# Chunk products of a state-space mixer placed in column groups of the array

## The chip, the cores and the metric

The kernel runs on one core of a Trainium2 chip. Its engines are TensorE (PE, with the weight loads shown apart as PEld), VectorE (DVE), ScalarE (ACT), GpSimd (POOL) and SyncE (SP, which issues most transfers). They run their own instruction streams in order and wait for each other by semaphores. The metric is the device time of one execution in microseconds; three timed runs of the kernel before gave 1025.63, 1027.56 and 1028.41 us, median 1027.56 us.

## The reference

One layer of a decoder for 512 tokens and 1024 features: a half-step SwiGLU, a mixer in which eight attention heads with forget gates and a diagonal state-space model (SSM) work side by side, a second half-step SwiGLU, a gated embedding and a final norm. The change is in the SSM alone: 32 groups of 16 channels, each with 64 complex states.

```python
abar_r = decay * jnp.cos(dt * ai)
abar_i = decay * jnp.sin(dt * ai)
...
bu_r = jnp.einsum('blgh,gph->blgp', u, bbar_r)
bu_i = jnp.einsum('blgh,gph->blgp', u, bbar_i)
...
_, _, xr, xi = lax.associative_scan(_ssm_combine, (a_r_full, a_i_full, bu_r, bu_i), axis=1)
y = (jnp.einsum('blgp,ghp->blgh', xr, c_re.astype(f32))
     - jnp.einsum('blgp,ghp->blgh', xi, c_im.astype(f32))
     + d_skip.astype(f32) * u)
y = jax.nn.gelu(y.reshape(B, L, SSM_WIDTH)).astype(s.dtype)
return y * jax.nn.sigmoid(y @ w_glu + b_glu)
```

## The kernel before

Most of the program is dense work: some 3800 matrix products of a 128x128 weight block with 512 columns (lines 236 to 238: each product of float32 numbers is three products of high and low parts), and some hundreds with 256 columns. `run` goes through a list of units. A unit has two steps, here called slots; in a slot ACT rounds the weights that are used two slots later to their high part `whi` (line 160), evictions and other chains issue their work, DVE makes the low part `wlo` (line 75), and PE does some twelve products. A unit's results are evicted in the next slot. Chains are generators. They are advanced twice in a slot, once ahead of the slot's products (their work for ACT and DVE) and once behind them (their work for PE), so that the code fixes each engine's order.

The SSM is computed in 64 chunks of 8 tokens. `ssm_prep` builds its matrices from the parameters during the first SwiGLU: `m1` (chunk inputs to states), `m2` (states to chunk outputs) and `m3` (chunk inputs to outputs of the same chunk). For `m3` it makes four batches of eight groups. In a batch, eight products (line 668) of a 16-column stationary block with 128 moving columns fill partitions 0 to 15 of two PSUM banks, two ACT copies (line 672) bring them to `kt`, and transfers spread `kt` to `m3`.

`ssm_chain` runs beside the products of the token units and the first query and key units. It turns the inputs into chunk form (line 720), multiplies to states (line 745: the two groups of a pair go to partitions 0 to 63 and 64 to 127 of the result), rotates and scans them on DVE (`rotate`, in two halves of 16 groups, whose last step is the four ACT copies `st` of line 788), and then treats four feature tiles of eight groups. `tile_chain` does this for a tile: `outputs` (16 products with 64 stationary columns and 128 moving ones, lines 797 and 798, in partitions 0 to 63 of two banks), `collect` (one bank copied by ACT, line 808, the other by DVE, line 810, to `yt`), `features` (eight transposes of 64 partitions, line 816), and the GELU in three parts (`gelu_a` begins with a copy on ACT, line 825). `TILES` lists the steps at which the four tiles begin: 4, 5, 7 and 8.

At these steps ACT and DVE have other work queued as well: the forget gate (`fz`, `fn`, `fc`, with a change of the activation table before and behind it), the values `v` of the attention (line 81 on ACT, line 78 on DVE), from whose PSUM banks the next unit takes its own, and then the queries, keys and softmax (`attention`).

Of the kernel before, what the change touches and what calls it, by code (L numbers as in the profile page):

```python
# [29 lines left out]
TILES = [4, 5, 7, 8]  # L30
# [12 lines left out]
def hybrid_trunk_kernel(ctx: ExitStack, tc: tile.TileContext, xT, pT, w13a, w2a, w13b, w2b, wqk, wv, ws, wf,  # L43
                        wglu, wout, wgate, wproj, cols, bf, ssm_s, ssm_bc, dskip, outT, dbg=None):
    nc = tc.nc
    V, S, G, T = nc.vector, nc.scalar, nc.gpsimd, nc.tensor
# [43 lines left out]
    # ---- constants  # L90
# [14 lines left out]
    # the activation table and the tensor engine's clock come up while x arrives  # L105
# [4 lines left out]
    # 0 | 1e30 above the diagonal  # L110
# [5 lines left out]
    # operands of the scores by head of the pair: (hi of q | selector of the head) and  # L116
    # (hi of k | cumulative gates of all heads), the head's own half of the partitions first
# [4 lines left out]
    # ---- dense work: a list of units; each has up to two weight halves of [128, 512], the matrix products that  # L122
    # use them in two steps, and what follows on the other engines
    class Unit:
        def __init__(self, srcs, steps, posts=(), need=None, alloc=None, ahead=True):
            # posts: (step it follows, slots to wait, function); need: what they wait for besides
# [47 lines left out]
    def run_posts(posts):  # L174
        # what waited for the first norm comes a few at a time
# [12 lines left out]
    def convert(u, nxt, h):  # L188
        # the next unit's half h of the weights, and what else is to be taken ahead
# [50 lines left out]
    def gemm_steps(box, key, rhs, n, half=None):  # L240
        # sum over n blocks of stationary weights against rhs(k) -> (hi, lo), in two steps; half: where both steps
        # find their weights, each in its own unit
# [11 lines left out]
    # ---- x*g -> hi, lo; squares summed; 1/rms by token  # L254
    class Norm:
# [36 lines left out]
        def scaled(self, src, scol, slots=2):  # L292
            # x*g/rms -> hi, lo, once the chain has run
# [41 lines left out]
    # ---- macaron half step  # L335
    PARTS = [range(0, 7), range(7, 14), range(14, 22)]

    def ffn_units(nrm, w13, w2, final, skip_first=False):
        units = []
        ready = lambda: nrm.r is not None  # L340
        for pi, part in enumerate(PARTS):
            hid = {}
            for f in part:
# [30 lines left out]
                if f == 0:  # L374
                    # side by side: the last blocks of the input come late
# [18 lines left out]
            # the first two go on side by side: the hidden parts that they need last come late  # L394
# [19 lines left out]
    # ---- SSM matrices from the parameters  # L414
    # "pair" layout: (group in pair, state) on partitions, 16 pairs on the free dim
    # "stack" layout: (real | imaginary, state) on partitions, 32 groups on the free dim
    def ssm_prep(M):
# [50 lines left out]
        # rotation tables e^{i phi c}, phi = 8 dt Im(a), c = 0..63  # L468
# [72 lines left out]
        # powers of abar, j = 0..8  # L541
# [7 lines left out]
        n = 1  # L549
# [17 lines left out]
        # zero-order-hold input matrix  # L567
# [46 lines left out]

        yield
        yield
        # chunk input matrices: [(s', h), (re | im, state)]
        m1 = []
        ps = None

# [940 lines left out]
```

## Time and profile before

| what | value |
|---|---|
| timed runs | 1025.63, 1027.56, 1028.41 us |
| profiled execution | span of 1025.1 us from the first to the last instruction; no other time of it is listed |
| PE, DVE, ACT busy | 99 %, 65 %, 41 % of the span |
| mean granted TensorE clock | 0.996 of full speed |

A busy share is an average over the whole span. The profile's row of the span in 40 slices shows where it differs: DVE is at nine tenths or more from about 460 to 540 us, and at five or six tenths in the long dense stretches. "PE busy" counts the time in which at least one product is under way; products overlap, so the time from the start of one to the start of the next is what counts. The chain of waits gives just that: in it each product has the time by which it delayed the end. A product of float32 operands with 128 or 64 columns shows as two records, called passes here, because the array goes over it twice; a transpose shows as one.

### The profile page before, as it was taken

The page shows a single profiled execution, that of the slowest core. Times are in us where ns is not written, and L with a number is a line of the kernel's source. Part 1 is how long each engine was busy: PE and PEld are TensorE (multiplying, and loading weights), DVE is VectorE, ACT ScalarE, POOL GpSimd, SP SyncE. Part 2 cuts the span into 40 slices and gives each one's busy share as a digit, 9 for nine tenths or more (in the row PEclk, how much of TensorE's full clock was granted, in tenths as well). Part 3 has the DMA queues.
Part 4 walks back from the last instruction along what each step waited for, and adds up shares of the span by engine and source line. Part 5 has one row for each costly group of instructions (what it writes and reads, how often), then busy time and mean ns, then how long its engine had stood idle before and what let it go on. Part 6 is the DMA issues. An engine that isn't in the chain of part 4 may idle for free.

```text
span 1025.1 us, 13779 instructions
## 1 busy us (share of the span) xinstructions
PE 1013.1 (99%) x5004; PEld 852.0 (83%) x5004; DVE 663.3 (65%) x1319; ACT 421.5 (41%) x793; POOL 45.6 (4%) x52
## 2 busy tenths in 40 slices
PE   9999999999999999999999999999999999999996
PEld 7888888888878889888888888888888888888896
DVE  6678687767645561879998975553455446655465
ACT  6333233322333352468897443332333224434332
POOL 0430000001000001001000000000000000000000
PEclk9999999999999999999999999999999999999998
DMA  6423332233244331212212232333333334533102
GB/s 207 151 88 96 108 96 93 77 99 103 83 105 117 103 92 52 63 53 83 73 52 75 88 96 86 100 88 100 100 103 88 98 103 150 168 93 104 32 1 82
DMA packets 58244, 96.06 MB, mean 94 GB/s; under 512 B 10224, under 2 KB 17008, under 8 KB 58176
## 3 DMA queue, kind: packets, MB, share of 16 engines
q1 hardware_dynamic: 57920, 94.63, 30.5%
q8 instruction: 39, 0.64, 0.3%
q0 software_dynamic: 256, 0.56, 0.2%
q14 instruction: 29, 0.24, 0.1%
HBM read 91.89 MB, written 2.10 MB: 92 GB/s over the span
## 4 chain that ended last, share of the span: by engine, by line
PE 96%; ACT 2%; DVE 1%; DMA 0%; SPq 0%; issue 0%; POOL 0%; DVEq 0%; ACTq 0%
PE ps L236 30%; PE ps L237 29%; PE ps L238 29%; PE ps L1439 1%; PE ps L797 1%; PE ps L668 1%; PE ps L798 1%; PE ps L1075 1%; PE ps L327 1%; PE ps L316 0%; ACT lg L81 0%; DMA x<-xT 0%; PE ps L1038 0%; PE ps L1039 0%; PE ps L745 0%; PE ps L1121 0%
## 5 line engine op out<-in xcount | busy, mean ns | idle before, releaser
L236 PE MATMUL ps<-xhl,whi 128*128 128x512 f32 x816 | 320.5, 393 | 0.0
L238 PE MATMUL ps<-xhl,whi 128*128 128x512 f32 x816 | 317.8, 389 | 0.0
L237 PE MATMUL ps<-xhl,wlo 128*128 128x512 f32 x816 | 317.8, 389 | 0.0
L160 ACT CAST whi<-wraw 128x512 fp32r<-128x512 f32 x324 | 196.1, 607 | 240.1 <-PE ps L238 177.8
L75 DVE TENSOR_TENSOR wlo<-wraw,whi 128x512 fp32r<-128x512 f32 x324 | 216.2, 673 | 11.0 <-ACT whi L160 10.7
L236 PEld LDWEIGHTS ps<-xhl,whi 128*128 128x128 f32 x816 | 153.2, 188 | 32.4 <-ACT kt L672 0.8
L238 PEld LDWEIGHTS ps<-xhl,whi 128*128 128x128 f32 x816 | 153.2, 188 | 32.2
L237 PEld LDWEIGHTS ps<-xhl,wlo 128*128 128x128 f32 x816 | 153.3, 188 | 31.0
L236 PE MATMUL ps<-h,whi 128*128 128x512 f32 x352 | 137.3, 390 | 0.0
L238 PE MATMUL ps<-h,whi 128*128 128x512 f32 x352 | 137.0, 389 | 0.0
L237 PE MATMUL ps<-h,wlo 128*128 128x512 f32 x352 | 137.0, 389 | 0.0
L78 DVE SCALAR_TENSOR_TENSOR x<-ps,x 128x512 f32<-128x512 f32 x48 | 33.2, 692 | 95.2 <-PE ps L238 95.1
L78 DVE SCALAR_TENSOR_TENSOR t<-ps,rbc 128x512 f32<-128x512 f32 x44 | 30.4, 690 | 78.0 <-PE ps L238 78.0
L236 PEld LDWEIGHTS ps<-h,whi 128*128 128x128 f32 x352 | 66.1, 188 | 13.7
L238 PEld LDWEIGHTS ps<-h,whi 128*128 128x128 f32 x352 | 66.1, 188 | 13.7
L237 PEld LDWEIGHTS ps<-h,wlo 128*128 128x128 f32 x352 | 66.1, 188 | 13.6
L75 DVE TENSOR_TENSOR t<-ps,rbc 128x512 f32<-128x512 f32 x44 | 30.4, 691 | 72.1 <-PE ps L238 65.9
L81 ACT ACTIVATE th<-t 128x512 f32<-128x512 f32 x44 | 27.8, 632 | 92.0 <-DVE t L75 92.0
L362 ACT CAST h<-t 128x512 fp32r<-128x512 f32 x44 | 27.4, 622 | 81.4 <-DVE t L75 81.4
L81 ACT ACTIVATE xhl<-x,colt 128x512 fp32r<-128x512 f32 x32 | 23.1, 725 | 46.7 <-DVE x L78 40.4
L236 PE MATMUL ps<-xhl,gw 128*128 128x256 f32 x128 | 36.5, 285 | 0.0
L238 PE MATMUL ps<-xhl,gw 128*128 128x256 f32 x128 | 36.2, 283 | 0.0
(255 smaller groups left out, 1165.2 us busy)
## 6 DMA issues: line engine op xcount, KB each, us to landing
wraw<-w13b SPq DMA_DIRECT2D x88, 256.0 KB, 2.9
wraw<-w13a SPq DMA_DIRECT2D x84, 256.0 KB, 2.9
wraw<-w2a SPq DMA_DIRECT2D x32, 256.0 KB, 2.7
wraw<-w2b SPq DMA_DIRECT2D x32, 256.0 KB, 2.7
wraw<-wqk SPq DMA_DIRECT2D x16, 256.0 KB, 2.8
wraw<-wout SPq DMA_DIRECT2D x16, 256.0 KB, 2.8
wraw<-wgate SPq DMA_DIRECT2D x16, 256.0 KB, 2.9
wraw<-w2a SPq DMA_DIRECT2D x16, 192.0 KB, 2.4
```

The source lines that it names most:

```text
L75: V.tensor_tensor(out, a, b, op)
L78: V.scalar_tensor_tensor(out, a, s, b, op0, op1)
L81: S.activation(out, in_, f, **kw)
L160: S.copy(hi[:, 0:n], w[:, 0:n])
L236: T.matmul(ps, lh, rh, start=start, stop=False)
L237: T.matmul(ps, ll, rh, start=False, stop=False)
L238: T.matmul(ps, lh, rl, start=False, stop=stop)
L327: T.matmul(ps[:, i * 128:(i + 1) * 128], rc[:, i:i + 1].to_broadcast([128, 128]), ident, start=True, stop=True)
L362: S.copy(hl[:, 0, :], box["t"])
L668: T.matmul(pss[gi // 4][0:16, (gi % 4) * 128:(gi % 4 + 1) * 128], bst[:, g, :], m2[q][:, gi, 0:8, :].rearrange("p t h -> p (t h)"), start= ...
L797: T.matmul(o, U[g // 16][:, g % 16, :], m3[g // 8][:, g % 8, :], start=True, stop=False)
L798: T.matmul(o, st[g // 16][:, g % 16, :], m2[g // 8][:, g % 8, 1:9, :].rearrange("p t h -> p (t h)"), start=False, stop=True)
```

## The change

Within `ssm_prep` the eight products of a batch go to four column groups of the array: group number gi lands in partitions 32 j to 32 j + 15 of one bank, with j = gi mod 4, and four ACT copies instead of two collect them. In `ssm_chain` two feature tiles are treated as one pair: the products of the first go to partitions 0 to 63, those of the second to 64 to 127, in turn. A pair is then collected by one ACT copy and one DVE copy of 128 partitions, transposed by eight full transposes into two banks, and each of its tiles gets its GELU input by two half copies, one on ACT and one on DVE. The pairs begin at steps 4 and 7. Comments were dropped elsewhere in the file, which shifts the line numbers.

```diff
@@ -27,7 +27,7 @@
 STATE = 1
-TILES = [4, 5, 7, 8]
+TILES = [4, 7]
 OUT = [[(0, 1), (2, 3), (4, 5), (6, 7)], [(0,), (1, 2), (6,), (3, 4), (7,), (5,)]]
...
@@ -655,21 +655,23 @@
...
 
         m3 = []
         for q in range(4):
             kt = g4([16, 8, 8, 16], base="kt")
             m = g4([128, 8, 128], base="m3")
             G.memset(m, 0.0)
             yield
-            pss = [bank(), bank()]
+            ps = bank()
             for gi in range(8):
-                g = q * 8 + gi
-                T.matmul(pss[gi // 4][0:16, (gi % 4) * 128:(gi % 4 + 1) * 128], bst[:, g, :],
+                i, j = divmod(gi, 4)
+                T.matmul(ps[32 * j:32 * j + 16, i * 128:(i + 1) * 128], bst[:, q * 8 + gi, :],
                          m2[q][:, gi, 0:8, :].rearrange("p t h -> p (t h)"), start=True, stop=True)
             yield
-            for i in range(2):
-                S.copy(kt[:, i * 4:i * 4 + 4].rearrange("p g t h -> p (g t h)"), pss[i][0:16, :])
+            for j in range(4):
+                S.copy(kt[:, j::4].rearrange("p g t h -> p g (t h)"),
+                       ps[32 * j:32 * j + 16, 0:256].rearrange("p (g x) -> p g x", g=2))
             s3 = [16, 8, 16]
             dd = tmp((16, 8, 16), "dd")
             tt(dd, dsk[:, q * 8:q * 8 + 8].unsqueeze(2).to_broadcast(s3),
...
@@ -788,22 +790,28 @@
                     S.copy(sh[i * 64:i * 64 + 64, g2::2, 1:64], p[2 * i][g2 * 64:g2 * 64 + 64])
             st.append(sh)
 
-        def outputs(ft):
+        def outputs(pr):
...
             pss = [bank(), bank()]
             for b in range(2):
                 for gi in range(4):
-                    g = ft * 8 + b * 4 + gi
-                    o = pss[b][0:64, gi * 128:(gi + 1) * 128]
-                    T.matmul(o, U[g // 16][:, g % 16, :], m3[g // 8][:, g % 8, :], start=True, stop=False)
-                    T.matmul(o, st[g // 16][:, g % 16, :], m2[g // 8][:, g % 8, 1:9, :].rearrange("p t h -> p (t h)"),
-                             start=False, stop=True)
+                    for k in range(2):
+                        for e in range(2):
+                            g = (2 * pr + e) * 8 + b * 4 + gi
+                            o = pss[b][e * 64:e * 64 + 64, gi * 128:(gi + 1) * 128]
+                            if k == 0:
+                                T.matmul(o, U[g // 16][:, g % 16, :], m3[g // 8][:, g % 8, :], start=True, stop=False)
+                            else:
+                                T.matmul(o, st[g // 16][:, g % 16, :],
+                                         m2[g // 8][:, g % 8, 1:9, :].rearrange("p t h -> p (t h)"),
+                                         start=False, stop=True)
             return pss
 
         def collect(pss):
-            yt = g4([64, 8, 8, 16], base="yt")
+            yt = g4([128, 8, 8, 16], base="yt")
             for b in range(2):
                 dst = yt[:, :, b * 4:b * 4 + 4, :].rearrange("p t g h -> p g t h")
-                src = pss[b][0:64].rearrange("p (g t h) -> p g t h", g=4, h=16)
+                src = pss[b].rearrange("p (g t h) -> p g t h", g=4, h=16)
                 if b == 0:
                     S.copy(dst, src)
                 else:
@@ -811,18 +819,21 @@
             return yt
 
         def features(yt):
-            ps = bank()
+            pss = [bank(), bank()]
             for t in range(8):
-                T.transpose(ps[:, t * 64:(t + 1) * 64], yt[:, t].rearrange("p g h -> p (g h)"), ident[0:64, 0:64])
-            return ps
+                T.transpose(pss[t // 4][:, (t % 4) * 128:(t % 4 + 1) * 128],
+                            yt[:, t].rearrange("p g h -> p (g h)"), ident)
+            return pss
 
         ge, ghl = out["ge"], out["ghl"]
 
-        def gelu_a(ft, ps):
-            if ft % 2 == 0:
+        def gelu_a(e, pss):
+            if e == 0:
                 out["yy"] = g4([128, 2, L], base="gel")
-            y = out["yy"][:, ft % 2]
-            S.copy(y.rearrange("p (c t) -> p c t", t=8), ps.rearrange("p (t c) -> p c t", t=8))
+            y = out["yy"][:, e]
+            for th, copy in enumerate((S.copy, V.tensor_copy)):
+                copy(y.rearrange("p (c t) -> p c t", t=8)[:, :, th * 4:th * 4 + 4],
+                     pss[th].rearrange("p (t e c) -> p e c t", t=4, e=2)[:, e])
             w = tmp(base="gw")
             act(w, y, AF.Square, scale=math.sqrt(0.044715))
             return y, w
@@ -839,38 +850,43 @@
             ghl.append(hl)
             defer(1, lambda: stt(hl[:, 1, :], y, 0.5, raw32(hl[:, 0, :]), MUL, SUB))
 
-        def tile_chain(ft):
...
-            pss = outputs(ft)
+        def tile_chain(pr):
...
+            pss = outputs(pr)
             yield
             yt = collect(pss)
             for _ in range(3):
                 yield
-            ps = features(yt)
-            yield
-            g = gelu_a(ft, ps)
-            yield
-            yield
-            gelu_b(*g)
-            yield
-            yield
-            gelu_c(*g)
-            yield
-
...
+            pss = features(yt)
+            yield
+            g0 = gelu_a(0, pss)
+            yield
+            yield
+            gelu_b(*g0)
+            g1 = gelu_a(1, pss)
+            yield
+            yield
+            gelu_c(*g0)
+            gelu_b(*g1)
+            yield
+            yield
+            gelu_c(*g1)
+            yield
...
         yield
         p = to_state(0)
         yield
         rots, tiles = {0: rotate(0, p)}, []
-        for i in range(max(TILES) + 7):
...
+        for i in range(max(TILES) + 8):
...
             for hf in rots:
                 for _ in range(ROT[hf].count(i)):
                     next(rots[hf], None)
             for c in tiles:
                 next(c, None)
             yield
...
             for c in tiles:
                 next(c, None)
             if i == STATE:
```

PE, the first batch of `m3`: `ps` is the result, `m2` the moving operand, `prepA` the stationary blocks. Before:

```order
L238 MATMUL ps_524_2576<-xhl_17_163,whi_508_2518 128x512
L668 MATMUL ps_525_2589<-m2_415_2092,prepA_45_304 16x128 x4
L668 MATMUL ps_526_2590<-m2_415_2092,prepA_45_304 16x128 x4
L236 MATMUL ps_524_2576<-xhl_18_168,whi_515_2546 128x512
L237 MATMUL ps_524_2576<-xhl_18_168,wlo_516_2547 128x512
```

And in the changed kernel:

```order
L238 MATMUL ps_524_2576<-xhl_17_163,whi_508_2518 128x512
L669 MATMUL ps_525_2589<-m2_415_2092,prepA_45_304 16x128 x8
L236 MATMUL ps_524_2576<-xhl_18_168,whi_515_2546 128x512
L237 MATMUL ps_524_2576<-xhl_18_168,wlo_516_2547 128x512
L238 MATMUL ps_524_2576<-xhl_18_168,whi_515_2546 128x512
```

The eight products stand at the same place; they now share one bank.

PE, the start of the first tile's products before (`U` holds the chunk inputs, `st` the states; `m3_519` and `m2_415` belong to the groups 0 to 7):

```order
L797 MATMUL ps_789_3904<-m3_519_2566,U_745_3667 64x128
L798 MATMUL ps_789_3904<-m2_415_2092,st_779_3852 64x128
L797 MATMUL ps_789_3904<-m3_519_2566,U_745_3667 64x128
L798 MATMUL ps_789_3904<-m2_415_2092,st_779_3852 64x128
L797 MATMUL ps_789_3904<-m3_519_2566,U_745_3667 64x128
```

The first pair's in the changed kernel (`m3_538` and `m2_437` belong to the groups 8 to 15):

```order
L803 MATMUL ps_785_3908<-m3_519_2566,U_741_3671 64x128
L803 MATMUL ps_785_3908<-m3_538_2659,U_741_3671 64x128
L805 MATMUL ps_785_3908<-m2_415_2092,st_775_3856 64x128
L805 MATMUL ps_785_3908<-m2_437_2194,st_775_3856 64x128
L803 MATMUL ps_785_3908<-m3_519_2566,U_741_3671 64x128
```

The products of the second tile, which stood a slot later, now stand between those of the first.

ACT, from the last states of the second half to the values `v` before:

```order
L788 COPY st_804_3975<-rc_802_3971 64x8x63 x2
L808 COPY yt_805_3983<-ps_798_3950 64x4x8x16
L160 CAST whi_809_4014<-wraw_776_3835 128x512
L825 COPY gel_811_4017<-ps_808_4005 128x512
L81 ACTIVATE gw_812_4019<-gel_811_4017 128x512
L81 ACTIVATE fn_806_3987<-fn_806_3987 8x512
L81 ACT_TABLE_LOAD
L81 ACTIVATE fn_806_3987<-fn_806_3987,half_87 8x512
L160 CAST whi_817_4066<-wraw_782_3865 128x512
L81 ACTIVATE v_819_4069<-ps_759_3749,rc_723_3534 128x8x64
```

And in the changed kernel:

```order
L790 COPY st_798_3977<-rc_796_3973 64x8x63 x2
L160 CAST whi_803_4014<-wraw_772_3839 128x512
L835 COPY gel_805_4017<-ps_801_4004 128x64x4
L81 ACTIVATE gw_806_4020<-gel_805_4017 128x512
L81 ACTIVATE fn_799_3986<-fn_799_3986 8x512
L81 ACT_TABLE_LOAD
L81 ACTIVATE fn_799_3986<-fn_799_3986,half_87 8x512
L160 CAST whi_810_4074<-wraw_778_3869 128x512
L81 ACTIVATE v_812_4077<-ps_755_3753,rc_719_3538 128x8x64
```

The copy of the second tile's products has left this place, and the copy `gel` is half as long; the rest stands as it did.

## Rows read from the trace of the kernel before

**Rows 1.** The page, busy time by engine and the granted clock in 40 slices.

```profile
PE 1013.1 (99%) x5004; PEld 852.0 (83%) x5004; DVE 663.3 (65%) x1319; ACT 421.5 (41%) x793; POOL 45.6 (4%) x52
PEclk9999999999999999999999999999999999999998
```

**Rows 2.** The page, shares of the chain that ended last.

```profile
PE 96%; ACT 2%; DVE 1%; DMA 0%; SPq 0%; issue 0%; POOL 0%; DVEq 0%; ACTq 0%
```

**Rows 3.** Chain of waits, first batch of line 668: start us, us, what.

```profile
276.66 1.85 PE ps L668 x16
278.51 0.43 PE ps L236
...
279.17 0.23 PE ps L238
```

**Rows 4.** Chain of waits, line 720's last transposes and line 745's first half.

```profile
411.48 0.22 PE ps L720 x2
...
413.54 2.02 PE ps L745 x64
```

**Rows 5.** Chain of waits, the first tiles' products and transposes.

```profile
431.64 0.36 PE ps L797 x2
...
435.28 0.43 PE ps L236
...
444.80 0.64 PE ps L816 x8
445.44 0.43 PE ps L236
...
452.71 0.43 PE ps L236
```

**Rows 6.** Groups by line, the copies of kt: busy us, mean ns | idle before.

```profile
L672 ACT COPY kt<-ps 16x512 f32<-16x512 f32 x8 | 4.6, 575 | 18.9 <-PE ps L668 18.9
```

**Rows 7.** Timeline of ACT: start us, us, instruction [idle before it <- what ended it].

```profile
441.17 2.48 ACT L788 COPY st<-rc 64x504 f32<-64x504 f32 x4 [6.50 <-DVE rc L75]
443.68 0.58 ACT L808 COPY yt<-ps 64x512 f32<-64x512 f32 x1
...
445.48 0.59 ACT L825 COPY gel<-ps 128x512 f32<-128x512 f32 x1 [0.57 <-PE ps L816]
446.10 0.63 ACT L81 ACTIVATE gw<-gel 128x512 f32<-128x512 f32 x1
...
449.70 1.24 ACT L81 ACTIVATE v<-ps,rc 128x512 fp32r<-128x512 f32 x2
```

**Rows 8.** Timeline of DVE in the same columns.

```profile
450.41 1.41 DVE L78 SCALAR_TENSOR_TENSOR v<-ps,rc,v 128x512 fp32r<-128x512 f32 x2 [4.73 <-ACT v L81]
...
452.75 0.68 DVE L810 COPY yt<-ps 64x512 f32<-64x512 f32 x1 [0.33 <-PE ps L798]
...
459.35 0.68 DVE L810 COPY yt<-ps 64x512 f32<-64x512 f32 x1 [0.43 <-PE ps L798]
460.59 1.38 DVE L75 TENSOR_TENSOR kcum<-fc,kcum 8x512 fp32r<-8x512 f32 x2 [0.56 <-ACT kcum L979]
462.00 0.69 DVE L75 TENSOR_TENSOR wlo<-wraw,whi 128x512 fp32r<-128x512 f32 x1
...
466.25 1.39 DVE L75 TENSOR_TENSOR qkhl<-qk,qkhl 64x512 fp32r<-64x512 f32 x2 [1.15 <-ACT qkhl L999]
```

**Rows 9.** Busy us of PE, PEld, DVE, ACT, POOL by stretch; clock, DMA, GB/s.

```profile
425.00:442.00 17.00, 17.00 (x107) 14.48 (x106) 16.77 (x29) 5.51 (x10) 0.00 (x0) 1.00 0.25 78
476.00:538.00 62.00, 61.84 (x326) 52.78 (x325) 60.38 (x185) 54.98 (x148) 5.61 (x8) 1.00 0.21 69
538.00:546.00 8.00, 6.65 (x38) 5.54 (x36) 7.86 (x23) 7.92 (x19) 0.00 (x0) 1.00 0.20 66
1010.00:1025.00 15.00, 6.66 (x55) 6.30 (x53) 6.24 (x16) 2.95 (x7) 2.10 (x3) 0.81 0.21 70
```

**Rows 10.** Waits of PE: who for whom, us in total, times, longest.

```profile
PE ps L1075 <- ACT pp L81: 1.5, 1, 1.5
```

## The prediction

> **What bounds the kernel now.** I read the shares by engine first, then the shares of the chain of waits, then the chain itself around the edited lines, and at last ACT and DVE there. PE is busy for 1013 of 1025.1 us, and the granted clock is full in every slice but the last [rows 1]. 96 % of the chain that ended last is PE [rows 2]: the end comes when PE is through its list, and a microsecond less of PE work is a microsecond gained unless PE has to wait for it later. So there are two questions: how much PE time goes, and whether the other engines can feed a PE that is earlier. For the second, see that DVE has 60.38 us of work in the 62 us from 476 to 538, that ACT and DVE fill the next 8 us while PE has only 6.65 us of work in them [rows 9], and that PE waits there for ACT, 1.5 us in one piece [rows 10]. In that stretch ACT and DVE are already as late as PE can bear.
>
> **Time of reference.** All terms come from the profiled execution, span 1025.1 us, the only time listed for it. The median of the timed runs, 1027.56 us, is 2.5 us above it. I take the sum off the median.
>
> **What a pass costs alone and side by side.** In a batch of line 668, 16 passes of 128 columns take 1.85 us; the first product behind them takes 0.43 us where a normal one takes 0.23 [rows 3]. A tile's 32 passes take 435.28 - 431.64 = 3.64 us [rows 5]. The first two take 0.36 us where a later pair takes 0.22, as two transposes of 128 columns do [rows 4, 5]. So a pass of 128 columns alone is 0.11 us, a block has 0.14 us at its start and 0.20 us at its end for changing the form of the array, and the width of the stationary block, 16 or 64, does not matter. Side by side is shown by one place only: line 745 puts 64 passes of 64 columns in turn into two column groups and takes 2.02 us [rows 4], 0.0316 us each, 0.063 us for two. Half of 0.11 us would be one such pass alone. So two side by side cost about 0.008 us over one alone. I carry this over: a round of two passes of 128 columns 0.118 us; a round of four 0.11 + 3 x 0.008 = 0.134 us.
>
> The Trainium skill ("TensorE: Matmul & The Clock Gate", What overlaps and what doesn't) says that a weight load overlaps products under way only where the row groups differ, and column groups share their rows; by that rule nothing here would run side by side. The trace disagrees: 0.0316 us for a pass of line 745. I keep the rule as a rival.
>
> **Batches of m3 (four times).** Before 1.85 us; after, four rounds of four, 4 x 0.134 = 0.54, and 0.10 at the start, 0.64 us. 1.21 us less, four times: 4.8 us. Bounds: nothing, if the groups take turns; 4 x (1.85 - 0.54) = 5.2 us, if rounds cost what one pass does. If only neighbours in the list pair up, eight rounds of 0.118 and 0.10, 1.04 us: 3.2 us. I take 4.8, nearest to the row of line 745. The number of ACT copies doubles; eight cost 0.575 us [rows 6], sixteen of half the length between 4.6 and 9.2 us in all, 0 to 4.6 us more, hidden, since ACT is at 41 % [rows 1] and nothing needs m3 before 431 us. If it were not hidden, a batch would cost up to 1.2 us more there.
>
> **Products of the tiles.** Before, four blocks of 3.64 + 0.20 = 3.84 us, 15.4 us. After, two blocks of 32 rounds: 32 x 0.118 + 0.14 + 0.20 = 4.1 us each, 8.2 us. 7.2 us less; bounds 0.6 us (all in turn, two blocks of 64 x 0.11 + 0.34 = 7.4 us) and 7.6 us (a round as cheap as a pass). A price for each turn from group to group, which would make it a loss, is excluded by line 745, which turns 64 times in 2.02 us.
>
> **Transposes.** Before, four blocks of 0.64 + 0.20 us [rows 5], 3.4 us. After, sixteen full ones of 0.11 us [rows 4], 1.8 us, in the form of the dense products, so without the change of form. 1.6 us less.
>
> PE's work falls by 4.8 + 7.2 + 1.6 = 13.6 us.
>
> **What passes through.** The 4.8 us come at 276 to 306 us, where DVE and ACT have room; everything behind moves with them. The other 8.8 us come between 431 and 467 us, and there the change moves PE but not what ACT and DVE do. I count in times of before, with the 4.8 us left aside.
>
> DVE has 16.77 us of work in the 17 us from 425 to 442 [rows 9]: the rotation of the second half, which does not depend on the tiles. So the last states are ready at 443.65, as before (441.17 + 2.48) [rows 7]. Behind them ACT has a fixed list up to the values v. From this list go the copy of line 808 (0.61 us to the next start), the 0.57 us of waiting for the transposes of line 816, and part of the copy of line 825 (half as long; 0.62 us to the next start, 0.4 after). v comes 1.4 us earlier, at 448.3 [rows 7], DVE's part of v at 449.0 instead of 450.41 [rows 8].
>
> PE in the meantime has lost the second tile's block (3.84 us), and 0.8 us of transposes, and has two blocks 0.26 us longer: 4.1 us, so it reaches 452.71 [rows 5] at 448.6. The unit that begins there takes its bank from the first v, free at about 449.7. PE waits 1.1 us: a new wait.
>
> DVE goes on from 449.0. Up to the start of wlo at 462.00 it had 11.6 us [rows 8]. The two waits for PE (0.33 and 0.43 us) and one copy of line 810 (0.6 us) go; a half copy (half of 0.68 us) comes; the wait for kcum on ACT stays or grows by some tenths. That is 10.7 us or a little more: 459.8, some 2.1 us early. PE, unhindered, would be 8 us early by then. It needs this wlo two slots on and must wait again, as for each later one.
>
> From here on DVE has next to no idle time up to 546 us, where PE was already waiting. It had 1.15 us at 466.25 [rows 8], part of which it can use, and it gets two more half copies (0.7 us). So of 8.8 us about 2.4 us are left behind 546 us; bounds 1.4 us (what ACT saves ahead of v) and 8.8 us (if ACT and DVE keep up after all).
>
> **Sum.** 4.8 + 2.4 = 7.2 us: 1027.56 - 7.2 = 1020.4 us.
>
> **The rivals.**
> 1. Neighbours only: four groups do no better than two, because a product's second pass stands ahead of the next product. For it: line 745 shows two groups, none shows four. Against it: two groups already overlap although each product has two passes. The batches give 3.2 us, in all 5.6: 1022.0 us.
> 2. No cap: ACT and DVE keep up, since their lists get shorter too and much of DVE's work waits for PE [rows 8]. Then all 13.6 us: 1014.0 us. Against it: the 1.5 us that PE waits at 546 us [rows 10].
> 3. Not side by side: the column groups take turns. PE saves 0.6 + 1.6 us at most, in the stretch where DVE and ACT cap it, and DVE has 0.7 us more: 1027.5 us, no change. It needs line 745 to be something else than overlap.
> 4. A tighter cap: the new waits eat all that the tiles gain, only the batches count: 1022.8 us.
> 5. Slower, by the clock. From 436 to 476 us PE would now wait in several pieces, some 6 us in all. In the last 15 us of the span PE has 6.66 us of work and its granted clock is 0.81 [rows 9]. If half of these 40 us ran at the lower of the two levels, 1.2 instead of 2.4 GHz, the mean would be 0.75 and PE lose 40 x (1/0.75 - 1) = 13 us: 1034 us. It decides from a mean of 0.85 on, where 7 us are lost. Against it: from 538 to 546 us PE is idle for 1.35 us and the clock stays at 1.00 [rows 9].
>
> **How the numbers follow.** A difference of 0.3 % (3.1 us) is about what a measurement of this kernel can tell from no change. Forecast 0.58, by itself between 1018 and 1022.5 us; neighbours only 0.12; no cap 0.12; not side by side 0.07; tighter cap 0.06; slower 0.05. The first, second, third and fifth of these are faster by over 0.3 %, 0.88 together; I take 0.02 off for one that stays just inside the bound: 0.86 faster, 0.09 within it, 0.05 slower. The range holds the forecast, the two rivals at 1022 and 1023, and the one at 1014 with its own spread: 1013 to 1024.5 us.
>
> **What the profile after would show.** Each batch as a piece of about 0.64 us in the chain of waits (1.04 for rival 1, 1.85 for rival 3); each pair's block about 3.9 us from its first pass to the next dense product (3.6 if perfect, over 7 if in turn); eight transposes in 0.88 us with no longer product behind them; a wait of PE of about 1 us for DVE's v at the first product behind the second pair, and more of them for wlo within the next 15 us; DVE's and ACT's stretch up to the softmax with less idle time than before; the granted clock at 1.00 there. The prediction is wrong if PE runs through these 40 us without waiting (then rival 2), if blocks come out at the length of two tiles, or if the dense products behind the batches wait for something that the 0.23 us of a normal one did not show.

## The result and the profile after

The changed kernel takes 1020.5 us (median of 4 runs, 1019.75 to 1021.53) where the kernel before takes 1027.39 us beside it (4 runs): the ratio is 0.9933, 95% interval [0.9922, 0.9945]. Forecast was 1020.4 us. The profiled execution of the changed kernel has a span of 1017.9 us, 7.2 us less than before.

The page of the changed kernel, busy time by engine, the granted clock in 40 slices, and the shares of the chain that ended last:

```profile
PE 1000.6 (98%) x4988; PEld 841.5 (83%) x4988; DVE 662.5 (65%) x1321; ACT 420.6 (41%) x799; POOL 44.7 (4%) x52
PEclk9999999999999999999999999999999999999998
PE 86%; DVE 7%; ACT 4%; issue 2%; DMA 1%; SPq 0%; POOLq 0%; POOL 0%; DVEq 0%; ACTq 0%
```

PE's share of the chain has fallen from 96 to 86 % [rows 2]; 7 % are now DVE and 4 % ACT. The end is no longer set by PE's list alone.

The chain of waits at the first batch of m3 (start us, us, what):

```profile
276.99 0.56 PE ps L669 x16
277.55 0.43 PE ps L236
```

The batch takes 0.56 us where it took 1.85, and the product behind it is as long as before [rows 3]: 1.29 us less, four times, 5.2 us.

The timeline of PE at the tiles (start us, us, instruction, idle before it and what ended it):

```profile
425.36 0.44 PE L803 MATMUL ps<-m,U 128*64 128x128 f32 x4
425.62 0.39 PE L805 MATMUL ps<-m,st 128*64 128x128 f32 x4
425.84 0.39 PE L803 MATMUL ps<-m,U 128*64 128x128 f32 x4
...
429.00 0.50 PE L236 MATMUL ps<-whi,xhl 128*128 128x512 f32 x1
...
443.51 0.50 PE L236 MATMUL ps<-xhl,whi 128*128 128x512 f32 x1 [1.52 <-DVE v L78]
...
449.10 1.03 PE L824 MATMUL ps<-ident,yt 128*128 128x128 f32 x8
449.89 0.48 PE L236 MATMUL ps<-xhl,whi 128*128 128x512 f32 x1
450.21 0.40 PE L237 MATMUL ps<-xhl,wlo 128*128 128x512 f32 x1
...
454.49 0.50 PE L237 MATMUL ps<-xhl,wlo 128*128 128x512 f32 x1 [1.39 <-DVE wlo L75]
...
461.48 0.50 PE L237 MATMUL ps<-xhl,wlo 128*128 128x512 f32 x1 [1.23 <-DVE wlo L75]
...
466.37 0.33 PE L1055 MATMUL ps<-qkhl,qkhl 128*128 128x128 f32 x1 [1.53 <-ACT qkhl L1026]
...
468.15 0.63 PE L237 MATMUL ps<-xhl,wlo 128*128 128x512 f32 x1
468.57 0.63 PE L238 MATMUL ps<-xhl,whi 128*128 128x512 f32 x1
```

Before, the first tile's block began at 431.57:

```profile
431.57 0.43 PE L797 MATMUL ps<-m,U 128*64 128x128 f32 x2
```

Three things stand here. A pair's block goes from 425.36 to 429.00, 3.64 us for 64 passes: four passes start every 0.22 us (each row with x4 is one such group), and two tiles take exactly what one took [rows 5]. The eight transposes and the product behind them take 1.11 us up to 450.21, of which 0.23 is the product: 0.88. And behind the blocks PE stops four times, for v, twice for wlo, and for qkhl; behind the last stop products begin 0.42 us apart and not 0.23, until 470.3. That last is the clock. By stretch, in the columns of [rows 9]:

```profile
380.00:396.00 16.00, 16.00 (x77) 15.92 (x77) 2.07 (x4) 2.96 (x5) 3.26 (x3) 1.00 0.25 82
...
464.00:480.00 16.00, 14.20 (x62) 11.56 (x61) 14.87 (x41) 13.62 (x32) 2.32 (x4) 0.89 0.29 95
...
470.00:530.00 60.00, 60.00 (x319) 51.66 (x318) 57.63 (x176) 52.75 (x143) 5.30 (x8) 1.00 0.21 67
```

The first two of these stretches in the kernel before:

```profile
380.00:396.00 16.00, 16.00 (x69) 15.17 (x69) 5.23 (x9) 3.62 (x6) 3.26 (x3) 0.89 0.32 95
464.00:480.00 16.00, 16.00 (x81) 13.20 (x80) 14.09 (x29) 15.42 (x32) 0.00 (x0) 1.00 0.25 82
```

Apart from its first and last microseconds, each kernel has one short stretch at the lower level, 1.2 GHz, in its profiled execution, and not in the same place: before at 391.7 to 394.7 us, behind 16 passes of one column each, the changed one at 467.2 to 470.3 us, behind the waits. From 470 to 530 us DVE is busy for 57.63 of 60 us, nearly as full as it was [rows 9].

The waits of PE in the changed kernel between 420 and 550 us (who for whom, us in total, times, longest):

```profile
PE ps L237 <- DVE wlo L75: 2.6, 2, 1.4
PE ps L1055 <- ACT qkhl L1026: 1.5, 1, 1.5
PE ps L236 <- DVE v L78: 1.5, 1, 1.5
PE ps L1091 <- ACT pp L81: 1.1, 1, 1.1
PE ps L1054 <- ACT kcum L1015: 0.3, 1, 0.3
```

Of these only the wait for pp was there before, with 1.5 us [rows 10] and 0.2 us more for mn just ahead of the same products. How the gain builds up and is given back shows when the 4176 dense products of the two traces are set side by side, each with its own counterpart (worked out from the starts in both traces):

```
start before, us   after minus before, us
 17.69                +0.33
306.42                -4.76   after the four batches
391.12                -4.74
400.43                -6.24   the kernel before was at the lower clock here
441.79                -9.94   after the first pair
466.45               -13.74   after the second pair and the wait for v
475.70                -7.97   after wlo twice, qkhl, and part of the slow stretch
500.00                -6.63   after the slow stretch
546.82                -7.79   after the wait for pp, and so to the last dense product
```

Behind the last dense product the changed kernel takes 0.6 us more than the kernel before (11.9 and 11.3 us), so that the spans differ by 7.2 us only. The slow stretch of the kernel before is worth 1.5 us in this table (from -4.74 to -6.24).

ACT and DVE where v is made, ACT's timeline first (start us, us, instruction, idle before it):

```profile
434.94 2.51 ACT L790 COPY st<-rc 64x504 f32<-64x504 f32 x4 [6.47 <-DVE rc L75]
...
442.00 1.24 ACT L81 ACTIVATE v<-ps,rc 128x512 fp32r<-128x512 f32 x2
```

and DVE's:

```profile
442.70 1.41 DVE L78 SCALAR_TENSOR_TENSOR v<-ps,rc,v 128x512 fp32r<-128x512 f32 x2 [3.79 <-ACT v L81]
...
452.33 1.38 DVE L75 TENSOR_TENSOR kcum<-fc,kcum 8x512 fp32r<-8x512 f32 x2 [1.21 <-ACT kcum L995]
453.74 0.69 DVE L75 TENSOR_TENSOR wlo<-wraw,whi 128x512 fp32r<-128x512 f32 x1
```

DVE's part of v comes at 442.70, 7.71 us earlier than before [rows 8]. 6.21 of these are the shift that the tiles' block already had (425.36 against 431.57), so the list up to v has become 1.5 us shorter. DVE then waits 1.21 us for kcum, and wlo follows at 453.74, 8.26 us earlier than before, 2.05 of them beyond the shift, while PE had come further than that: hence the 1.39 us at 454.49.

### The profile page after: what moved, and what is told of

It reads as the page before. It is cut to its first block, busy times and chain, and to the rows that moved or that the text cites. A ratio compares the mean times of both kernels' runs of the same rounds, so it can differ in the third digit from the quotient of the medians.

```text
span 1017.9 us, 13762 instructions
## 1 busy us (share of the span) xinstructions
PE 1000.6 (98%) x4988; PEld 841.5 (83%) x4988; DVE 662.5 (65%) x1321; ACT 420.6 (41%) x799; POOL 44.7 (4%) x52
## 4 chain that ended last, share of the span: by engine, by line
PE 86%; DVE 7%; ACT 4%; issue 2%; DMA 1%; SPq 0%; POOLq 0%; POOL 0%; DVEq 0%; ACTq 0%
PE ps L236 28%; PE ps L238 27%; PE ps L237 27%; DVE wlo L75 1%; ACT lg L81 1%; DVE rot L75 1%; DVE lg L1067 1%; PE ps L1455 1%; DVE rc L75 1%; DMA x<-xT 1%; DVE pb L75 1%; PE ps L327 1%; DVE qkhl L75 1%; PE ps L316 0%; ACT whi L160 0%
```

## The experiments

All ratios are to the kernel before, run beside the kernel on the same chip. Kernels that are told with the same "before" ran together.

**The batches alone.** The kernel before with the edit of the batches (products and copies of `kt`) and nothing else:

```
-            pss = [bank(), bank()]
+            ps = bank()
...
+                i, j = divmod(gi, 4)
+                T.matmul(ps[32 * j:32 * j + 16, i * 128:(i + 1) * 128], bst[:, q * 8 + gi, :],
...
```

> The four batches of m3 in four column groups, the feature tiles as before. Theory (all that the batches save passes through, the tiles' gain is mostly eaten by ACT and DVE): 0.56 us a batch instead of 1.85, and 5.1 us off the end, 0.5 %. Rival A (PE bounds everywhere, so the tiles bring most of the 7 us): also 5.1 us here. Rival B (the softmax stretch, where PE already waited 1.5 us, swallows gains that come ahead of it): under 2 us off the end, and a longer wait of PE for ACT at the end of the softmax stretch.

Measured 1021.49 us, before 1027.5, ratio 0.9937 [0.9924, 0.9950]. The batch is 0.56 us as in the full change, PE has no new wait, and behind the batches the dense products come 5.1 us earlier than before, counted from the first one of each trace. (The kernel before ran its slow stretch at 392 us in that trace, this one did not, which makes 6.5 at the last dense product.) The gain passes through whole; a swallowed one is out. By the traces it is 5.1 us; the 6.0 us between the medians lie above that.

**The pairs alone.** The changed kernel with the batches as before:

```
-            ps = bank()
+            pss = [bank(), bank()]
...
-                T.matmul(ps[32 * j:32 * j + 16, i * 128:(i + 1) * 128], bst[:, q * 8 + gi, :],
+                T.matmul(pss[gi // 4][0:16, (gi % 4) * 128:(gi % 4 + 1) * 128], bst[:, g, :],
```

> The feature tiles in pairs, the batches of m3 as before. Theory: PE's work falls by about 8.5 us there, but PE waits for v, wlo, kcum and qkhl for over 5 us, and 1 to 2.5 us are left at the end. Rival A (PE bounds): 7 to 8.5 us off the end, no new waits. Rival C (the pairs bring nothing at all, the whole change is the batches): 0 us, within 0.5.

Measured 1026.1 us, ratio 0.9983 [0.9975, 0.9992], 1.4 us less. Its waits:

```profile
PE ps L237 <- DVE wlo L75: 2.6, 2, 1.4
...
PE ps L236 <- DVE v L78: 1.5, 1, 1.5
PE ps L1054 <- ACT qkhl L1025: 1.5, 1, 1.5
```

The same waits as in the full change. The two parts add about up: 6.0 and 1.4 us against 6.9. Counted from the first dense product of each trace PE is 7.5 us ahead behind the second pair and has 1.5 us of that left at the last one; both traces have the slow stretch at 392 us, and this one has another from 474 us on, which is part of what was lost.

**Tile after tile.** The changed kernel with the loop over the two tiles outside, so that 32 passes in a row go to one column group and then 32 to the other:

```
-            for b in range(2):
-                for gi in range(4):
-                    for k in range(2):
-                        for e in range(2):
+            for e in range(2):
+                for b in range(2):
+                    for gi in range(4):
+                        for k in range(2):
```

> The changed kernel, but in each pair all products of the first tile stand ahead of those of the second, so that neighbours in the list use the same column group. Theory: nothing runs side by side, a pair's block takes about 7.1 us instead of 3.6, PE's work grows by 7 us, and since PE waits over 5 us for ACT and DVE right behind, the end comes only 0 to 2.5 us later than in the changed kernel. Rival A (PE bounds): 7 us later. If the blocks stay at 3.6 us, the order in the list does not matter and the queue of PE looks far ahead.

Measured 1023.92 us, ratio 0.9961 [0.9948, 0.9974]. PE's timeline at the first block:

```profile
426.34 0.43 PE L803 MATMUL ps<-m,U 128*64 128x128 f32 x2
426.61 0.38 PE L805 MATMUL ps<-m,st 128*64 128x128 f32 x2
...
429.44 0.44 PE L803 MATMUL ps<-m,U 128*64 128x128 f32 x4
429.66 0.44 PE L805 MATMUL ps<-m,st 128*64 128x128 f32 x4
...
433.09 0.50 PE L236 MATMUL ps<-whi,xhl 128*128 128x512 f32 x1
```

The block takes 6.75 us instead of 3.64: two passes every 0.22 us, and four only at the seam (the rows with x4), where passes of both tiles stand in the list together. So it is the order of the list that makes the overlap. Some 6.2 us of PE work more cost 3.4 us against the changed kernel; my theory had 0 to 2.5, a PE that is the bound 7. Neither holds: about half of it falls into time in which PE would wait anyway. The wait for v is gone, one of the two for wlo too, the one for qkhl remains.

**The same group twice running.** The changed kernel with the batch's products listed 0 0 1 1 2 2 3 3 by column group instead of 0 1 2 3 0 1 2 3:

```
-                i, j = divmod(gi, 4)
+                j, i = divmod(gi, 2)
...
-                S.copy(kt[:, j::4].rearrange("p g t h -> p g (t h)"),
+                S.copy(kt[:, 2 * j:2 * j + 2].rearrange("p g t h -> p g (t h)"),
```

> The changed kernel, but in the batches of m3 two neighbours in the list go to the same column group (0 0 1 1 2 2 3 3). Theory (the groups run side by side as far as PE looks ahead in its list, which is only a few products): 0.7 to 1.1 us a batch instead of 0.56, 0.6 to 2 us on the end. Rival D (each group has a queue of its own, however the list is ordered): 0.56 us a batch, no change. Rival E (a group must be empty before the next product in the list may start): over 1.5 us a batch.

Measured 1021.34 us, ratio 0.9936 [0.9922, 0.9951]. The chain of waits at the batch:

```profile
277.01 0.58 PE ps L669 x16
```

0.58 us against 0.56: my theory, in which only near neighbours in the list overlap (0.7 to 1.1), fell, and so did rival E (over 1.5). Rival D's 0.56 nearly came, but that the list may be ordered in any way is out by the kernel above. With four passes of one group in a row the others still start; with 32 they don't. How far ahead passes are let start lies between, as far as the two kinds of block can be compared (four groups of 16 columns here, two of 64 there).

**No logarithm.** The changed kernel without the logarithm in the forget gate (a copy in its place, so two loads of an activation table of 1.28 us go on either side):

```
-            act(zn, zn, AF.Ln, scale=0.5, bias=half[0:8])
+            act(zn, zn, AF.Copy, scale=0.5)
```

> The changed kernel without the logarithm of the forget gate (a scaled copy stands in its place), so that ACT loads no other activation table and loads none back, 2 x 1.28 us less in its list between the last states and the tiles' second GELU. Theory (ACT's list ahead of v sets when PE goes on behind the second pair): v comes about 1.3 us earlier, PE's wait for v (1.5 us) is gone, the later waits for wlo and qkhl (4.1 us together) shrink, and the end comes 1 to 2.5 us earlier than in the changed kernel. Rival F (DVE's amount of work up to the end of the softmax is the cap, ACT is not): within 0.5 us of it, the waits move to later places.

Measured 1019.78 us, before 1027.15, ratio 0.9925 [0.9911, 0.9938]. Its waits:

```profile
PE ps L237 <- DVE wlo L75: 2.6, 2, 1.4
...
PE ps L1091 <- ACT pp L81: 1.5, 1, 1.5
PE ps L1055 <- ACT qkhl L1026: 1.5, 1, 1.5
```

The wait for v is gone, the others have not moved, and pp costs 0.4 us more. Its median is 7.4 us under its kernel before, the changed kernel's 6.9, and the 0.5 us between them go with the clock: in the two runs with a mean clock of 0.997 it took 1018.51 and 1018.98 us, in those with 0.993 and 0.994 1020.58 and 1020.73, no less than the changed kernel at that clock (1019.75 to 1021.53). The rival holds: at that clock the wait for v was worth nothing by itself, and my 1 to 2.5 us fell. Whether the clock stayed up in two of four runs because that wait was gone, four runs can't tell.

**State copies on GpSimd.** The changed kernel with ACT's four copies st of the second half on GpSimd:

```
-                    S.copy(sh[i * 64:i * 64 + 64, g2::2, 1:64], p[2 * i][g2 * 64:g2 * 64 + 64])
+                    (S.copy if hf == 0 else G.tensor_copy)(sh[i * 64:i * 64 + 64, g2::2, 1:64], ...)
```

> The changed kernel with the four copies of the second half's states on GpSimd instead of ACT. ACT then does not stand still for 6.5 us for DVE's rotation, and v can come when PE has its sums, about 439.5 instead of 442.0 us. Theory: PE's wait for v is gone, the following ones are shorter, 1 to 2.5 us earlier than the changed kernel, unless GpSimd's copies (0.7 us each by its casts) make PE wait for the states. Rival F (DVE's amount of work is the cap): within 0.5 us.

Measured 1021.65 us, ratio 0.9940 [0.9926, 0.9953]: nothing gained. GpSimd's timeline, the copies:

```profile
436.55 4.28 POOL L790 COPY st<-rc 64x504 f32<-64x504 f32 x4 [47.80 <-PE ps L824]
```

and ACT's:

```profile
440.44 0.63 ACT L81 ACTIVATE gw<-gel 128x512 f32<-128x512 f32 x1 [3.50 <-DVE gel L835]
...
444.04 1.24 ACT L81 ACTIVATE v<-ps,rc 128x512 fp32r<-128x512 f32 x2
```

ACT was free 2.5 us earlier, and stood 3.50 us waiting for DVE's half of gel. v is not earlier: 444.04, in the changed kernel 442.00; 1.4 of these 2.0 us are a slow stretch at 387 us, which this trace has and that of the changed kernel has not. PE also waits 0.4 us for GpSimd's copies. So ACT's list was not what held v alone: DVE is as late.

**Low parts on GpSimd.** The changed kernel, where every second wlo of the queries, keys and GLU is made by GpSimd:

```
-            tt(lo[:, 0:n], w[:, 0:n], raw32(hi[:, 0:n]), SUB)
+            (G if u.pool and i == 1 else V).tensor_tensor(lo[:, 0:n], w[:, 0:n], raw32(hi[:, 0:n]), SUB)
```

> The changed kernel with every second low part of the weights wlo of the query, key and GLU units made by GpSimd instead of DVE: some ten instructions of 0.6 us leave DVE between 431 and 546 us. Theory (ACT's list ahead of v, then DVE and ACT in turns): the waits for wlo (2.6 us) are gone, that for v and that for qkhl stay, 1 to 3 us earlier than the changed kernel if GpSimd takes about 1.4 us for one (0.72 for half the size). Rival G (ACT alone sets the end of the softmax stretch): within 0.5 us.

Measured 1019.17 us, ratio 0.9918 [0.9905, 0.9932], the fastest of the kernels that compute the whole reference: 1.3 us under the changed one, though the intervals overlap and two of its four runs had a mean clock of 0.995, which the changed kernel had in none. Its waits:

```profile
PE ps L1055 <- ACT kcum L1016: 1.7, 1, 1.7
PE ps L1056 <- ACT qkhl L1027: 1.6, 1, 1.6
...
PE ps L237 <- DVE v L78: 1.5, 1, 1.5
...
PE ps L238 <- DVE wlo L165: 0.8, 1, 0.8
```

Less DVE work shortens the waits for wlo from 2.6 to 1.0 us, and 1.4 us of that come back at kcum. At the end of the two traces 0.7 to 0.9 us are left, under the 1 to 3 that I expected.

**Both.** The two edits above together:

> Both together: the second half's states and every second wlo of these units on GpSimd. Theory: the gains add in part, 2 to 4.5 us earlier than the changed kernel, 1016 to 1018.5 us; PE's waits in the stretch fall below 2 us. Rivals F and G: no better than the better one of the two.

Measured 1019.28 us, ratio 0.9923 [0.9909, 0.9936]: no better than the one edit, and it has the wait for v at 2.0 us. PE's waits in the stretch are 6.2 us in all, not under 2, and my 2 to 4.5 us fell.

**The same relief for both kernels.** The single edits showed that a wait that is taken away comes back later. So I took the work of DVE and ACT away over the whole stretch, with PE's list untouched, from the changed kernel and from the one before. The low parts of the weights of the forget gate, values, queries, keys and GLU are not computed (their products take the high parts again), nor is the logarithm:

```
-            lo = pool.tile([128, 512], F32R, name=nm("wlo"), tag="wlo", bufs=4)
+            lo = hi if u.zero else pool.tile([128, 512], F32R, name=nm("wlo"), tag="wlo", bufs=4)
...
-            tt(lo[:, 0:n], w[:, 0:n], raw32(hi[:, 0:n]), SUB)
+            if not u.zero:
+                tt(lo[:, 0:n], w[:, 0:n], raw32(hi[:, 0:n]), SUB)
...
-            act(zn, zn, AF.Ln, scale=0.5, bias=half[0:8])
+            act(zn, zn, AF.Copy, scale=0.5)
```

> The changed kernel with work taken off DVE and ACT in the stretch from 425 to 546 us, PE's list untouched: for the weights of the forget gate, the values, the queries and keys and the GLU the low parts are not computed (25 DVE instructions wlo of 0.6 to 0.68 us between 425 and 546 us, some 15 us; their products take the high parts again), and the logarithm of the forget gate is left out. Theory (what holds back the tiles' gain is the amount of work of DVE and ACT in that stretch): the waits for v, wlo, kcum and qkhl go or become small, the gain is no longer given back from 452 us on, and this kernel is 3 to 6 us faster than the changed one, 1014.5 to 1017.5 us; against the kernel before with the same relief it is 10.5 to 13.6 us faster. Rival G (the order of the dependent steps, rotation, states, tiles, v, scores, sets the pace, whatever the amount of work): PE waits at the same places for v, kcum and qkhl, and only the 2.6 us for wlo go, most of which come back as other waits; 1018.5 to 1020 us, and against the kernel before with the same relief 7 to 8 us.

> The kernel before with the same work taken off DVE and ACT: no low parts of the weights of the forget gate, the values, the queries and keys and the GLU (their products take the high parts again), no logarithm. Both theories: PE hardly waited before, so at most the 1.5 us at 546 us go: 1025.5 to 1027.5 us. It is the partner of the changed kernel with the same relief; their difference is what tells the theories apart (10.5 to 13.6 us, or 7 to 8).

Measured 1014.87 us for the changed one, ratio 0.9876 [0.9861, 0.9891], and 1024.93 for the one before, 0.9971 [0.9959, 0.9982] (before beside them 1028.14). The difference is 10.06 us where it is 6.9 without relief: between the 10.5 that my theory had at least and the 8 that the rival had at most, close to the theory. The kernel before gained 3.2 us where I had 1.5 at most. The changed kernel with relief, PE's waits:

```profile
PE ps L1057 <- ACT qkhl L1028: 1.6, 1, 1.6
...
PE ps L1056 <- issue: 0.4, 1, 0.4
```

and by stretch:

```profile
430.00:464.00 34.00, 32.03 (x198) 26.55 (x197) 24.81 (x49) 25.54 (x46) 0.00 (x0) 0.99 0.18 62
464.00:480.00 16.00, 16.00 (x77) 13.40 (x76) 12.44 (x42) 12.85 (x35) 2.33 (x4) 0.91 0.32 102
```

v, wlo and pp hold PE no longer; the 2.0 us at the first scores stay, and so does a slow stretch behind them (0.91). From 430 to 464 us DVE and ACT are idle for a quarter of the time, but not right ahead of the scores. ACT waits last at 451.76, and then works without a break up to the copies qkhl, which the scores wait for (ACT's timeline, and the stretch from 452 to 462 us in the columns of [rows 9]):

```profile
451.76 0.63 ACT L81 ACTIVATE ghl<-gel 128x512 fp32r<-128x512 f32 x1 [1.48 <-DVE gel L78]
...
461.24 1.26 ACT L1028 CAST qkhl<-qk 64x512 fp32r<-64x512 f32 x2
```

```profile
452.00:462.00 10.00, 8.03 (x36) 6.29 (x34) 7.43 (x13) 9.75 (x19) 0.00 (x0) 1.00 0.17 62
```

The relief took 16.5 us off DVE's busy time (662.5 to 646.0 us) and 1.9 off ACT's (420.6 to 418.7), by the logarithm and its table loads ahead of these 10 us. So this wait does not show that the order of the steps alone holds the scores: ACT's amount of work ahead of them was left as it was. The dense products of the two relieved traces are 15.5 us apart at 467 us and 11.4 at the end. The relief itself is worth 5.7 to 5.9 us in the trace of the changed kernel and 2.0 to 2.3 in the one before (the waits for pp and mn, 1.7 us there, go): some 3.5 us more for the changed one. This counts also that PE no longer needs the low parts at all, for which it waited 2.6 us: the relief takes away work and these waits together, and no run parts them.

Now the account of the tiles: PE's list is 9.3 us shorter there (7.7 for the blocks, 1.6 for the transposes). In the two traces without relief 1.5 of it is left (8.1 from the first to the last dense product, less 5.1 of the batches and 1.5 of the slow stretch at 392 us), as in the trace of the pairs alone. Of the 7.8 us that are lost, what the relief took away, nearly all of it DVE's, accounts for some 3.5, the wait at the first scores, behind ACT's full list, for 2.0, and 3 us at half the clock for about 1.4; 0.9 us I can't place.

**What the clock does to the runs.** Each run is listed with its mean granted clock. In the 17 runs of the kernel before that stood beside the first four experiments, and in the others:

```
kernel             clock          us
before             0.997          1026.03 to 1026.29 (5 runs)
before             0.995          1026.53 to 1027.29 (3)
before             0.994          1027.50 to 1029.13 (5)
before             0.993          1028.74 to 1029.25 (4)
changed            0.993, 0.994   1019.75 to 1021.53 (4)
batches alone      0.997          1020.23 (1)
batches alone      0.995          1021.38 to 1022.05 (4)
pairs alone        0.993          1026.00 to 1026.75 (8)
pairs alone        0.994, 0.995   1025.19 to 1025.78 (3)
```

The kernel before spreads over 3 us with the clock. The changed kernel has 0.993 or 0.994, the clock of the slowest runs of before, in all four. At 0.993 the pairs alone gain 2.8 us on the kernel before (1026.15 against 1028.97, the medians of these runs) and not 1.4; their one run at 0.995 gains 1.3 on the median of before at 0.995. Alike means are not like histories, though: the batches alone have 0.995 in a profiled execution that is at 1.00 both from 380 to 396 us and from 464 to 480, and at 0.69 from 1004 to 1020; the kernel with low parts on GpSimd has 0.995 with 0.89 from 464 to 480. So 2.8 us is no clean price of the pairs without the slow stretch. The traces give about the same, 1.5 us left and 1.4 lost by the stretch, 2.9 in all. That the slow stretch behind the new waits keeps the clock down is argued and not shown: the window from 464 to 480 us has 0.89 in the profiled execution of every kernel with the pairs or tiles in column groups, but for the one without the logarithm (1.00, in a run with a mean of 0.997, and with the waits for wlo and qkhl in place) and the relieved one (0.91), and 1.00 in the three kernels without them. The stretch follows the waits in most executions, then, not in all. No run kept the waits and forbade the stretch.

## Why the prediction was right

The sum was 7.2 us against 6.9 measured. Its terms one by one:

- **Side by side.** Right, and a little better than taken. The round of two costs what one pass costs (0.109 us, against 0.118), and so does the round of four (0.56 us a batch against 0.64). The terms were 4.8 and 7.2 us; they are 5.2 by the chain of waits (5.1 between the dense products) and, by 2 x (2 x 3.84 - 3.84), 7.7. The upper bounds were the true values. Line 745, from which I took 0.008 us for each further pass, has other passes, of 64 columns, and the surcharge did not carry over. Rivals 1 and 3 are out.
- **The rule of the Trainium skill** ("TensorE: Matmul & The Clock Gate", What overlaps and what doesn't): by it a weight load would wait where the row groups are the same. In the batch all 16 passes use the same rows, their weight loads are recorded with 0.096 us each and the passes with 0.273, and all are through in 0.56. The trace disagrees with the rule, for four column groups now too. It did so for the dense products already: PE is busy for 1013 us and PEld for 852 of the same 1025 [rows 1]. That by this one sentence nothing at all would run side by side was the prediction's own reading of it.
- **Transposes.** Right: 0.88 us for eight and no longer product behind them, 1.6 us less.
- **Batches pass through.** Right; shown by the batches alone. The sixteen copies of `kt` take 0.364 us each, 5.8 us in all, 1.2 us more than the eight, and hold nothing up.
- **v 1.4 us earlier, PE waits 1.1 us.** Measured 1.5 and 1.52. PE was further ahead by the better blocks.
- **wlo 2.1 us early, and PE waits again.** Measured 2.05 us, 1.39 and 1.23 us of waiting.
- **Of 8.8 us about 2.4 are left.** PE's list is 9.3 us shorter. Measured 1.4 in the times of the pairs alone and 1.5 in the traces, 2.8 against runs of the same mean clock of 0.993. The mechanism holds, but not wholly as I told it: I let the amount of work of DVE and ACT take all the rest. By the relief, nearly all of it DVE's, it took about 3.5 us with the waits for wlo; the first scores took 2, which ACT's list there explains as well as their order, and no run tells the two apart; and the clock took 1.4. Rival 2 is out by the new waits, rival 4 by the pairs alone, whose ratio of 0.9983 [0.9975, 0.9992] is clear of 1.
- **The clock, rival 5.** It occurred in small. I had 40 us at a mean of 0.75, or nothing; the window from 464 to 480 us has 0.89, 3 us at the lower level, and it cost about 1.4 us. That the granted clock would be at 1.00 there, a sign named in the prediction, was wrong. The working against it, one wait at 538 us with the clock at 1.00 [rows 9], was one case; four waits within 23 us were another.

So the close agreement is in part luck, errors of opposite sign: 0.4 us more from the batches, some 0.4 more from the tiles with the slow stretch left aside, and about 1.4 less by the clock. That makes 6.6 us; the other 0.3 lie within the spread of the runs.

## What to carry to other kernels

List small products for different column groups in turn: here two or four groups cost PE what one costs, and putting one group's 32 passes ahead of the other's loses nearly all of it. Before counting such a gain, ask at each place where the PE time goes away whether the other engines can bring their operands earlier: where they had room the gain came through whole, where they were full 1.4 of 9.3 us did (about 2.9 but for the slow stretch of the clock). When a wait is taken away, look at the next one on the list before believing its price: here it took over most of the price each time, and only less work for the full engines over the whole stretch moved the end by more. Such a relief tells of the engines that it relieves and of no other: look which list is still full at the waits that stay.

## What was not expected of the hardware

- Four column groups of 16 columns run at the pace of one: 16 passes of 128 columns in 0.56 us (1.85 in one group), with four in a row for one group in 0.58.
- The granted clock can be at the lower level for some 3 us behind 16 passes of one column, or behind waits, and is not so in every execution: in the same code, from 380 to 396 us, it was 0.89 in six of the twelve profiled kernels and 1.00 in the others. Over the runs of one kernel a mean clock of 0.993 to 0.997 goes with 3 us in 1027, and the mean does not say where the lower level lay.
- A strided copy of 64x504 takes 1.07 us on GpSimd (4.28 for four) and 0.63 on ACT (2.51 for four).
